# Weight slots, weight halves and work tiles moved to other places modulo 256 bytes in a one-core two-block transformer

## The chip, the cores and the metric

The kernel runs on one core of one Trainium2 chip, in one launch. The metric is the device time of that core in microseconds (us). A profiled execution gives one trace; the plain times are from executions of the same program.

## The reference

Two transformer blocks of depth 2 follow each other on one sequence of 256 tokens and width 1024, all in float32. Cut to the order of the sublayers:

```python
def first_block(x, ...):                     # layer 0 even, layer 1 odd
    mix = even_mixer(...) or odd_mixer(...)  # mLSTM + neighbourhood, or differential attention
    x = layer_norm(ALPHA * x + mix)
    x = layer_norm(ALPHA * x + memory_cross_attention(x, mem, wq, wkv, wo))   # 4 heads of 256
    x = layer_norm(ALPHA * x + swiglu(x, w_gu, w_down))                       # hidden 2816
def second_block(x, ...):                    # twice
    x = layer_norm(ALPHA * x + 0.5 * swiglu_ffn(x, w_in, w_out))              # hidden 2816
    x = layer_norm(ALPHA * x + mixer_sublayer(...))       # top-k, stick-breaking, convolution, gates
    x = layer_norm(ALPHA * x + memory_cross_attention_2(...))                 # 4 heads of 128
    x = layer_norm(ALPHA * x + 0.5 * swiglu_ffn(x, w_in, w_out))
```

Nearly all arithmetic is products of the 256 activations with weight matrices: 725 units of 128x1024 weights, each used once.

## The kernel before

**Split products.** Every weight and every activation of a large product is held as two parts of a reduced float type, high and low; a product is three matmuls (high by high, low by high, high by low). `Stream._load` brings a unit of 128x1024 float32 by a DMA of SP's queue into one of 4 stage tiles; `Stream._split` makes the parts from it: a cast on ScalarE (L218) for the high half, a subtraction on VectorE (L219) for the low one. Both halves lie in one of 10 slots of the pool `wp`, 8192 bytes each in a partition. The order of all engines' work is written out by the program itself, with a table of pauses; nothing is scheduled by a planner.

**Two operands.** In `matmul(out, a, b)` the first operand stands in TensorE's array (it is loaded by a weight load, engine PEld in the profile), the second streams through it (engine PE). A large matmul here streams 256 or 512 columns against a standing 128x128. While one streams, the load for the next one runs. In the profile's rows the streaming operand is named first (`ps<-xT,w` streams `xT`).

**Who is what.** The large products are of these kinds, and the starts in a partition modulo 256 bytes are those of the built program (all other offsets inside a tile are multiples of 512 bytes):

| product (lines) | streams, at | stands, at | standing minus streaming |
|---|---|---|---|
| units, `unit_group` (L348, L350, L352) | `xT`, 128 | weights, 192 | +64 |
| output projections, `bg_mm` (L417) | weights, 192 | `ph`, `pl`, 0 | +64 |
| memory keys, `kv_k` (L307 to L309, `w` by `w`, 256 columns) | memory, 192 | weights, 192 | 0 |
| memory values, `kv_v` (`w` by `w`, 512 columns) | weights, 192 | memory, 192 | 0 |
| `vproj` (512 columns), first step of `ffn` (256 columns) | weights, 192 | `xT`, 128 | -64 |
| branches of `mixer` (`ph` by `w`) | `ph`, `pl`, 0 | weights, 192 | -64 |

`xT` holds the two parts of the activations, 8 blocks of 256 columns each; `ph` and `pl` are the two parts of an intermediate, in tiles of the pool `a1` (35 tiles of 1 KB, tag `k1`), which also holds most other small work tiles.

**The feed-forward sublayer** (`ffn`, six times) matters most below. Four units of the first step come first; one pair of hidden blocks is turned by transposes (L595). Then `for j in range(2, 22)` takes two units of 24 matmuls (gate and up), makes `h` and its parts, and for 16 of the `j` also one block of the output projection with the parts of two steps before (`bg_both`, 24 matmuls of L417 over five accumulators, three of them 512 columns wide). In the first such block each of these three is opened by one 512-wide matmul, so that it has 21 matmuls; all others of these blocks are 256 wide:

```python
for c in [lo] if start or stop else range(lo, hi, 256):
    e = hi if start or stop else c + 256
    mm(acc[:, c - lo:e - lo], p, z[:, c:e], start=start, stop=stop)
```

The last six blocks are held back for `bg_tail`, where the sublayer's normalisation runs between them.

Of the kernel before, what the change touches and what calls it, by code (L numbers as in the profile page):

```python
# [9 lines left out]
F32 = mybir.dt.float32  # L10
F32R = mybir.dt.float32r
# [156 lines left out]

class Blank:


# [16 lines left out]
class Stream:  # L190
# [20 lines left out]
    def _split(self):  # L211
        n = self.net
        cols = self.plan[self.split][2]
        w = self.stage.pop(self.split)
        both = n.wp.tile([128, 2048], F32R, tag="w2", name="w2")
        hi, lo = both[:, :1024], both[:, 1024:]
        self._low()
        n.nc.scalar.copy(hi[:, :cols], w[:, :cols])  # L218
        self.due = lambda: n.nc.vector.tensor_sub(lo[:, :cols], w[:, :cols], hi[:, :cols].bitcast(F32))  # L219
        self.parts[self.split] = (hi, lo)  # L220
        self.split += 1
        self.live += 1
# [44 lines left out]
class Net:  # L267
# [1241 lines left out]
    def build(self):  # L1509
        nc, tc = self.nc, self.tc  # L1510
        with ExitStack() as ctx:
            pool = lambda name, bufs, **k: ctx.enter_context(tc.tile_pool(name=name, bufs=bufs, **k))
            self.one = pool("one", 1)
            self.stage = pool("stage", STAGE)
            pad = pool("pad", 1).tile([128, 16], F32, name="pad")
            self.wp = pool("wp", W_SLOTS)
            wide = pool("a2", 18)
            self.act = Multi(pool("a1", 35), wide) if self.real else Blank()
            self.small = SmallMix(pool("sm_col", 24), pool("sm_o", 2)) if self.real else Blank()
            self.psum = pool("psum", 8, space=bass.MemoryType.PSUM)  # L1520
            self.dram = pool("dram", 1, space=bass.MemoryType.DRAM)
            ctx.enter_context(tc.manual_schedule())
            sq = self.one.tile([128, 3, 128], F32, name="sq")
            self.xT = [self.one.tile([128, 8, S], F32R, tag=f"xT{i}", name="xT") for i in range(2)]
            xq = [self.k2(name="xq") for _ in range(4)]
            for u in range(4):
                nc.scalar.dma_start(xq[u], self.a["xT"][u // 2, :, (u % 2) * 512:(u % 2) * 512 + 512]
                                    .rearrange("p (k c) -> p k c", k=2))
            self.xq = xq
            self.ws.start()  # L1530
            nc.sync.dma_start(sq, self.a["c_sq"])
            self.ident, self.negt, self.strict = (sq[:, i, :] for i in range(3))
            self.mhalf = self.one.tile([128, 8], F32, name="mhalf")
            nc.vector.memset(self.mhalf, -0.5)
            self.negone = self.one.tile([128, 128], F32, name="negone")
            nc.vector.memset(self.negone, -1.0)

            subs = [self.even,
                    lambda: self.xattn("x0", "memT", 2, 1),
                    lambda: self.ffn("f0", 2, 2 * ALPHA, 4 * EPS),  # L1540
                    self.odd,
                    lambda: self.xattn("x1", "memT", 2, 4),
                    lambda: self.ffn("f1", 5, 2 * ALPHA, 4 * EPS)]
            for l in range(2):
                b = 6 + 4 * l
                subs += [lambda l=l, b=b: self.ffn(f"h{l}0", b, 4 * ALPHA, 16 * EPS),
                         lambda l=l, b=b: self.mixer(l, b + 1),
                         lambda l=l, b=b: self.xattn(f"y{l}", "memT2", 1, b + 2),
                         lambda l=l, b=b: self.ffn(f"h{l}1", b + 3, 4 * ALPHA, 16 * EPS)]
            if self.start:  # L1550
                for u in range(4):
                    self.x_split(u)
                self.late_loads()
                self.lam_load()
                self.rel_load()
                for _ in self.tables():
                    pass
            for f in subs[self.start:self.stop]:
                f()
            if self.stop < 14:  # L1560
                self.flush()
                for t in range(2):
                    nc.sync.dma_start(self.out[0, t * 128:t * 128 + 128, :], self.x[:, t, :])
# [40 lines left out]
```

## Time and profile before

| | |
|---|---|
| median of 3 runs | 2245.8 us (2245.5 to 2246.91) |
| the profiled execution: its time, its span | 2246.46 us, 2244.7 us |
| TensorE matmuls, share of the span | 98%, 17920 instructions |
| VectorE, ScalarE, GpSimd | 67%, 51%, 9% |
| granted TensorE clock | 0.998 of full speed (2.4 GHz) |
| DMA, share of 16 engines | about 56%, 182 GB/s |

The span is the time from the first to the last instruction of the trace; the time of the execution is 1.8 us longer. Matmuls are pipelined, so the duration of one (some 280 ns) is much longer than the distance from one start to the next, here called the pitch; the pitch is what the time is made of.

### The profile page before, as it was taken

What the parts mean: (1) busy time and instruction counts of PE and PEld (TensorE: products, weight loads), DVE (VectorE), ACT (ScalarE), POOL (GpSimd) and SP (SyncE); (2) the same over time, 40 slices, a digit from 0 to 9 for tenths busy, and PEclk for the clock granted to TensorE, in tenths of its full rate; (3) what the DMA queues carried; (4) which work ended last, traced back from release to release, by engine and by line L of the source; (5) the groups of instructions that cost most, each with busy time, mean ns of one, the idle gap of its engine ahead of it and who ended that gap; (6) DMA issues with size and microseconds to landing.
All of it is one profiled execution on the core that took longest, in us unless ns stands there. A gap on an engine that the chain in (4) does not pass through costs nothing.

```text
span 2244.7 us, 43647 instructions
## 1 busy us (share of the span) xinstructions
PE 2207.1 (98%) x17920; PEld 2127.7 (95%) x17920; DVE 1498.5 (67%) x2270; ACT 1154.3 (51%) x1844; POOL 203.1 (9%) x239
## 2 busy tenths in 40 slices
PE   8999999999999999999999999999999999999998
PEld 6999999998989999999899999999999999998998
DVE  5885666676657667656587667657656587677665
ACT  4555454378545444444845554444543845545542
POOL 0720000011000000000211100000000101100000
PEclk9999999999999999999999999999999999999999
DMA  7754476463446664764465655764764545554762
GB/s 228 179 170 159 168 256 189 155 209 135 162 152 224 200 188 161 234 189 151 141 182 166 207 179 175 234 191 139 254 190 145 165 153 181 178 193 164 254 191 75
DMA packets 118090, 407.67 MB, mean 182 GB/s; under 512 B 14169, under 2 KB 19418, under 8 KB 117890
## 3 DMA queue, kind: packets, MB, share of 16 engines
q1 hardware_dynamic: 116258, 402.00, 55.0%
q0 software_dynamic: 768, 1.57, 0.9%
q8 instruction: 140, 2.29, 0.4%
q10 hardware_dynamic: 864, 1.31, 0.2%
q14 instruction: 60, 0.49, 0.1%
HBM read 403.76 MB, written 1.06 MB: 180 GB/s over the span
## 4 chain that ended last, share of the span: by engine, by line
PE 84%; DVE 4%; ACT 4%; DMA 4%; issue 2%; POOL 1%; ACTq 0%; SPq 0%; DVEq 0%; POOLq 0%
PE acc L417 21%; PE ps L348 15%; PE ps L350 14%; PE ps L352 14%; PE ps L307 4%; PE ps L309 4%; PE ps L308 4%; DVE w L219 2%; ACT w L218 2%; PE ps L558 1%; PE ps L737 1%; DMA w<-in_o_qk 1%; DMA xq<-in_xT 1%; PE ps L757 1%; ACT qr L1115 0%
## 5 line engine op out<-in xcount | busy, mean ns | idle before, releaser
L219 DVE TENSOR_TENSOR w<-w,w 128x1024 fp32r<-128x1024 f32 x725 | 885.6, 1240 | 364.4 <-ACT w L218 360.5
L348 PE MATMUL ps<-xT,w 128*128 128x256 f32 x3232 | 903.0, 279 | 0.0
L350 PE MATMUL ps<-xT,w 128*128 128x256 f32 x3232 | 896.5, 277 | 0.0
L352 PE MATMUL ps<-xT,w 128*128 128x256 f32 x3232 | 896.1, 277 | 0.0
L218 ACT CAST w<-w 128x1024 fp32r<-128x1024 f32 x725 | 748.6, 1050 | 232.2 <-PE ps L352 121.7
L348 PEld LDWEIGHTS ps<-xT,w 128*128 128x128 f32 x3232 | 607.2, 188 | 8.1 <-issue 5.1
L352 PEld LDWEIGHTS ps<-xT,w 128*128 128x128 f32 x3232 | 608.9, 188 | 0.0
L350 PEld LDWEIGHTS ps<-xT,w 128*128 128x128 f32 x3232 | 607.5, 188 | 0.6
L417 PE MATMUL acc<-w,ph 128*128 128x256 f32 (+1 forms) x2966 | 496.9, 283 | 2.1 <-ACT ph L292 1.5
L417 PEld LDWEIGHTS acc<-w,ph 128*128 128x128 f32 x2966 | 421.1, 189 | 7.6 <-ACT ph L292 2.3
L417 PE MATMUL acc<-w,pl 128*128 128x256 f32 (+1 forms) x1462 | 330.1, 284 | 2.3 <-DVE pl L293 2.3
L417 PEld LDWEIGHTS acc<-w,pl 128*128 128x128 f32 x1462 | 238.5, 189 | 2.7 <-DVE pl L293 2.7
L529 POOL TENSOR_TENSOR col<-col,mhalf 128x1 f32<-128x1 f32 (+1 forms) x38 | 28.6, 751 | 1554.7 <-DVE col L537 1308.3
L570 ACT ACTIVATE k<-ps 128x256 f32<-128x256 f32 x120 | 46.0, 383 | 155.7 <-PE ps L352 155.6
L292 ACT CAST ph<-k 128x256 fp32r<-128x256 f32 x120 | 48.8, 406 | 133.4 <-DVE k L572 133.4
L307 PE MATMUL ps<-w,xT 128*128 128x256 f32 (+1 forms) x304 | 102.0, 336 | 9.2 <-ACT w L218 9.2
L308 PE MATMUL ps<-w,xT 128*128 128x256 f32 (+1 forms) x304 | 99.5, 327 | 1.2 <-DVE w L219 1.2
L571 DVE SCALAR_TENSOR_TENSOR k<-k,ps 128x256 f32<-128x256 f32 x120 | 50.4, 420 | 75.0 <-ACT k L570 74.9
L309 PE MATMUL ps<-w,xT 128*128 128x256 f32 (+1 forms) x304 | 99.3, 327 | 0.0
L307 PE MATMUL ps<-w,w 128*128 128x256 f32 (+1 forms) x288 | 96.0, 333 | 0.0
L544 ACT ACTIVATE x<-x,col 128x512 f32<-128x512 f32 x28 | 20.3, 724 | 141.1 <-POOL col L529 109.5
L309 PE MATMUL ps<-w,w 128*128 128x256 f32 (+1 forms) x288 | 91.9, 319 | 0.0
(259 smaller groups left out, 2268.4 us busy)
## 6 DMA issues: line engine op xcount, KB each, us to landing
w<-in_h_g SPq DMA_DIRECT2D x160, 512.0 KB, 4.5
w<-in_h_d SPq DMA_DIRECT2D x88, 512.0 KB, 4.5
w<-in_f_g SPq DMA_DIRECT2D x80, 512.0 KB, 4.4
w<-in_m_gate SPq DMA_DIRECT2D x48, 512.0 KB, 4.2
w<-in_f_d SPq DMA_DIRECT2D x44, 512.0 KB, 4.5
gb<-in_ln_row SPq DMA_DIRECT2D x28, 512.0 KB, 6.9
w<-in_m_c SPq DMA_DIRECT2D x24, 512.0 KB, 3.5
w<-in_m_br SPq DMA_DIRECT2D x24, 512.0 KB, 3.9
```

What stands on the lines that cost most here:

```text
L218: n.nc.scalar.copy(hi[:, :cols], w[:, :cols])
L219: self.due = lambda: n.nc.vector.tensor_sub(lo[:, :cols], w[:, :cols], hi[:, :cols].bitcast(F32))
L292: nc.scalar.copy(hi, src)
L307: mm(ps, a[0], b[0], start=first, stop=False)
L308: mm(ps, a[0], b[1], start=False, stop=False)
L309: mm(ps, a[1], b[0], start=False, stop=last)
L348: mm(ps, ws[i][0][:, k, :], xh[:, k, :], start=k == 0, stop=False)
L350: mm(ps, ws[i][1][:, k, :], xh[:, k, :], start=False, stop=False)
L352: mm(ps, ws[i][0][:, k, :], xl[:, k, :], start=False, stop=k == 7)
L417: mm(acc[:, c - lo:e - lo], p, z[:, c:e], start=start, stop=stop)
L570: nc.scalar.activation(h, pg, AF.Tanh, scale=0.5)
L571: nc.vector.scalar_tensor_tensor(h, in0=h, scalar=1.0, in1=pg, op0=OP.add, op1=OP.mult)
```

## The change

The spacer of 64 bytes ahead of the weight slots goes. A slot grows from 8192 to 8448 bytes, 33 times 256. In a slot the halves begin at its start, or, for units of the names in `BESIDE`, 64 bytes further. `a1` has 34 tiles for 35. No operation is added or taken away, and on every engine the built program has the same instructions in the same order; only some waits of ScalarE and VectorE in the gate stage of `mixer` (L1418, L1378, L292, L293, L218) name an earlier or later release of a work tile, about 50 in all.

```diff
+HALF = 16
+BESIDE = {"b", "a", "g", "qk", "q", "k", "qa", "ckv", "iq", "ik", "s", "c", "gate", "t"}
+def beside(name):
+    return name.split("_", 1)[-1] in BESIDE
...
-        both = n.wp.tile([128, 2048], F32R, tag="w2", name="w2")
-        hi, lo = both[:, :1024], both[:, 1024:]
+        off = HALF if beside(self.plan[self.split][0]) else 0
+        both = n.wp.tile([128, 2048 + 4 * HALF], F32R, tag="w2", name="w2")
+        hi, lo = both[:, off:off + 1024], both[:, off + 1024:off + 2048]
...
-            pad = pool("pad", 1).tile([128, 16], F32, name="pad")
             self.wp = pool("wp", W_SLOTS)
             wide = pool("a2", 18)
-            self.act = Multi(pool("a1", 35), wide) if self.real else Blank()
+            self.act = Multi(pool("a1", 34), wide) if self.real else Blank()
```

In the built program the slots begin at 128 modulo 256, the `a1` tiles at 192; `xT` stays at 128. The table of above becomes:

| product | streams, at | stands, at | standing minus streaming, before and now |
|---|---|---|---|
| units | `xT`, 128 | weights, 192 | +64, +64 |
| output projections | weights, 128 | `ph`, `pl`, 192 | +64, +64 |
| memory keys | memory, 128 | weights, 192 | 0, +64 |
| memory values | weights, 128 | memory, 128 | 0, 0 |
| `vproj` | weights, 128 | `xT`, 128 | -64, 0 |
| first step of `ffn` | weights, 192 | `xT`, 128 | -64, -64 |
| branches of `mixer` | `ph`, `pl`, 192 | weights, 128 | -64, -64 |

Between two products the load of the next one's standing operand runs while the last matmul of the one before streams. From a unit to an output block that pair was 128 and 0 (+128) and is now 128 and 192 (+64); from an output block to a unit it was 192 and 192 (0) and is now 128 and 192 (+64). Seen modulo 512, all slots lay alike before; now every second slot lies 256 bytes off the others.

## Rows read from the trace of the kernel before

**Rows 1.** Page: the span, and busy time, share and instructions by engine.

```profile
span 2244.7 us, 43647 instructions
PE 2207.1 (98%) x17920; PEld 2127.7 (95%) x17920; DVE 1498.5 (67%) x2270; ACT 1154.3 (51%) x1844; POOL 203.1 (9%) x239
```

**Rows 2.** TensorE's waits: total us, times, longest; first and last of 15.

```profile
PE ps L307 <- ACT w L218: 9.2, 2, 7.2
...
PE ps L1104 <- ACT oz L1100: 0.2, 1, 0.2
```

**Rows 3.** Groups of matmuls by line and shape: count, busy us, mean ns.

```profile
L348 PE MATMUL ps<-xT,w 128*128 128x256 f32 x3232 | 903.0, 279 | 0.0
...
L307 PE MATMUL ps<-w,w 128*128 128x256 f32 x192 | 56.2, 293 | 0.0
...
L307 PE MATMUL ps<-w,xT 128*128 128x512 f32 x112 | 47.0, 420 | 9.2 <-ACT w L218 9.2
```

**Rows 4.** L348 in two stretches: count, min/median/max ns, first and last start.

```profile
L348 PE MATMUL ps<-xT,w x60: 276/276/276, 408.4 to 428.5; 128*128 128x256 f32 x60
...
L348 PE MATMUL ps<-xT,w x45: 281/281/281, 469.8 to 485.4; 128*128 128x256 f32 x45
```

**Rows 5.** Timeline: first and last L348 of both (in the second, 44th).

```profile
408.42 0.28 PE L348 MATMUL ps<-xT,w 128*128 128x256 f32 x1
...
428.48 0.28 PE L348 MATMUL ps<-xT,w 128*128 128x256 f32 x1
...
469.83 0.28 PE L348 MATMUL ps<-xT,w 128*128 128x256 f32 x1
...
485.02 0.28 PE L348 MATMUL ps<-xT,w 128*128 128x256 f32 x1
```

**Rows 6.** Timeline: twelve memory keys, then ten each of vproj and memory values.

```profile
118.71 0.28 PE L307 MATMUL ps<-w,w 128*128 128x256 f32 x1
...
120.03 0.28 PE L309 MATMUL ps<-w,w 128*128 128x256 f32 x1
...
455.06 0.39 PE L307 MATMUL ps<-w,xT 128*128 128x512 f32 x1
...
457.12 0.39 PE L307 MATMUL ps<-w,xT 128*128 128x512 f32 x1
...
202.82 0.39 PE L307 MATMUL ps<-w,w 128*128 128x512 f32 x1
...
204.86 0.39 PE L307 MATMUL ps<-w,w 128*128 128x512 f32 x1
```

**Rows 7.** L417: an output block of ffn, then a stretch of another tail.

```profile
L417 PE MATMUL acc<-w,ph x12: 281/281/281, 330.3 to 332.2; 128*128 128x256 f32 x12
...
L417 PE MATMUL acc<-w,ph x24: 276/276/276, 152.8 to 156.7; 128*128 128x256 f32 x24
```

**Rows 8.** The two units behind that output block (333:337.8), by line.

```profile
L348 PE MATMUL ps<-xT,w 128*128 128x256 f32 x15 | 4.1, 276 | 0.0
```

**Rows 9.** First block: behind its first, second and third wide matmul (280.2:282.7).

```profile
L417 PE MATMUL acc<-w,pl 128*128 128x256 f32 x2 | 0.4, 276 | 0.0
...
L417 PE MATMUL acc<-w,pl 128*128 128x256 f32 x2 | 0.4, 281 | 0.0
...
L417 PE MATMUL acc<-w,ph 128*128 128x256 f32 x6 | 1.1, 281 | 0.0
```

**Rows 10.** Loop of ffn behind its first block, two of six: length, matmuls.

```profile
282.74:428.82 146.08, 146.08 (x1275) 1.00 0.66 215
...
696.03:842.11 146.08, 146.08 (x1274) 1.00 0.68 214
```

**Rows 11.** Gate stage of the first mixer (1167:1280), by line and shape.

```profile
L350 PE MATMUL ps<-xT,w 128*128 128x256 f32 x186 | 51.7, 278 | 0.0
```

**Rows 12.** L1418: ScalarE's idle time before it; who waited (us, times).

```profile
  PE ps L352: 25.5, 25
...
  PEld ps L307: 0.7, 2
```

## The prediction

> **What bounds the kernel now.** The page comes first. TensorE's matmuls fill 98% of the span, VectorE 67%, ScalarE 51% [rows 1]. The list of waits says how much of the rest could be had back: TensorE waits 15 times for someone, from 9.2 us down to 0.2 us, 30 us in all [rows 2]. So neither DMA nor the engines that split the weights set the time; the pitch of 17920 matmuls does, on average 2244.7/17920 = 125 ns. The change does not touch their number or order, so it can act only on the pitch, or through the few waits that it moves.
>
> The next view is one line in two stretches that nothing interrupts. The same instruction, L348, with the same shape and the same starts modulo 256 (streaming at 128, standing at 192), takes 276 ns each time in one stretch and 281 ns each time in the other [rows 4]. The timeline gives the pitches [rows 5]: 20.06 us over 59 x 3 = 177 matmuls is 113.3 ns; 15.19 us over 43 x 3 = 129 is 117.8 ns. I call these the quick and the slow step. The reader is to see the minimum, median and maximum: 60 of 60 alike, 45 of 45 alike. A uniform stretch does not change its step by itself; whichever it comes in with, it keeps. The duration tells which it is.
>
> Third, the places where the step does change. In the loop of `ffn` an output block (L417) runs at 281 ns, yet elsewhere the same line runs 24 times at 276 ns [rows 7], so L417 is not slow by nature. The two units behind the block are at 276 ns again [rows 8]. So in each round the step turns slow on entering the output block and quick on leaving it. These are the places where the distance of the two operands modulo 256 is another for one matmul: +128 on entering, 0 on leaving, +64 everywhere else. The first block shows a third kind of place: behind its first 512-wide matmul the step is quick, behind the second slow, behind the third slow [rows 9]. A wide matmul met in the quick step leaves the slow one, and one met in the slow step leaves the slow one; the first differs, but there the +128 came just before.
>
> **The change, part by part.**
>
> *Output blocks and units.* After the change, entering and leaving have +64 as well, and all of it lies at 128 and 192, where L348 shows both steps holding [rows 4]. What turned the step slow on entering is gone, and so is what turned it quick on leaving. Then the step of the whole loop is decided once, in the first block. There the first wide matmul is met quick (without the +128 ahead of it) and should leave the slow step, as the second one does now; the second and third keep it. If the units before came in slow, the result is the same. Behind this block no 512-wide matmul follows until the tail, so I expect the rest of the loop to stay slow.
>
> The price: behind its first block the loop has 19 x 48 + 15 x 24 = 1272 matmuls (19 pairs of units, 15 output blocks); the window of 146.08 us counts three more that overlap its ends [rows 10]. That is 114.84 ns each, and the second loop has the same length to 0.01 us, as do three more. All slow: 1272 x 117.8 = 149.8 us, 3.75 us more. All quick: 1272 x 113.3 = 144.1 us, 1.95 us less. For six feed-forward sublayers: +22.5 or -11.7 us. I take +22.5. The first block itself has the same mixture and the tail is entered slow either way: nothing for either.
>
> *Memory keys.* Both operands lie alike (0) and the pitch is 1.32 us over 11, 120.0 ns [rows 6]. There are 3 x 192 = 576 such matmuls [rows 3]. At +64 they are at one of the two steps: 576 x 2.2 = 1.3 us gained if slow, 576 x 6.7 = 3.9 us if quick. I take the middle, -2.5 us.
>
> *`vproj`.* Its distance goes from -64 to 0. It has 2.06 us over 9, 228.9 ns, now; memory values, also 512 wide and at 0, have 2.04 over 9, 226.7 ns [rows 6]. 3 x 112 = 336 matmuls [rows 3] by 2.2 ns: -0.7 us. The other bound is no gain. Memory values, the first step of `ffn` and the branches keep their distance: nothing.
>
> *Units outside the loops.* 3 x 3232 [rows 3] less 6 x 912 leaves 4224. Where they follow branches, attention or stalls, either step may hold, and the change alters some of what precedes them. In the gate stage their mean is 278 ns [rows 11], so 2 parts in 5 are slow. All quick would be 4224 x 0.4 x 4.5 = -7.6 us, all slow 4224 x 0.6 x 4.5 = +11.4 us. Nothing says which way; I take zero and keep both ends.
>
> *34 tiles and the moved waits.* About 50 waits of ScalarE and VectorE in the two gate stages change their releaser, among them GpSimd's additions. ScalarE is idle before L1418 for 25.5 us because it waits for TensorE's unit itself, and TensorE has lost 0.7 us to it [rows 12]. That idle time hides a work tile released a round or two earlier. Were the cover gone, the branch matmuls behind that activation would wait; I take zero, and twice the present loss, 1.4 us, as the other end.
>
> *The splits.* Casts and subtractions write to other places; VectorE and ScalarE have a third and a half of the span free [rows 1]. Zero.
>
> Sum: 22.5 - 2.5 - 0.7 = +19.3 us. Against the profiled execution's own time (span 2244.7 and 1.8 around it, 2246.5) that is 2265.8; the median of the runs lies 0.7 below that execution, so 2265. Slower by 0.9%. A measurement of this kernel tells about 0.2%, 4.5 us, from no change.
>
> The Trainium skill, in "SBUF — State Buffer", section "Who interferes with whom", gives TensorE two independent read ports, one for the streaming operand and one for the weight load, and says that "PE and ACT never wait on anyone". By that rule where operands lie cannot matter, and the sum would be zero, 2246 us. The rows differ: 113.3, 117.8 and 120.0 ns for the same shape [rows 5, 6]; the measurement decides here, though that the place causes the difference is my reading of them.
>
> **The rivals.**
>
> *The loop locks quick: 2230 us, faster.* The mechanism is the same, with one step the other way: the wide matmuls of the first block, met at the new places, leave the quick step behind. Then each loop saves 1.95 us, 11.7 us in six; memory keys at the quick step give 3.9 and `vproj` 0.7: 2245.8 - 16.3 = 2229.5. For it: L417 can hold the quick step [rows 7], and one wide matmul did leave it quick [rows 9]. Against it: the second, met quick, did not. It decides at one point, the step of the matmuls right behind the third wide one.
>
> *Places repeat over more than 256 bytes: about 2248.* All slots lie alike modulo 512 now; with a slot of 33 times 256 bytes every second one lies 256 off. If that counts, every new unit is a place where the step can change, and distances come up that no row of this trace shows. With half the matmuls of the loops at either step, the mean is 115.55, 7632 x 0.7 = +5.3 us; less the 3.2 us of the keys and `vproj`, +2. The ends are wide: -11.7 from the loops if all is quick, and 7632 x (120.0 - 114.84) = +39 if all is as the keys are now. It falls to either side.
>
> *The place does not matter, and both steps have another cause: 2246.* For it: the same places show both steps [rows 4]. Against it: the change of step falls on the same places in each round, and five loops have the same length within 0.01 us.
>
> **How the numbers follow.** The forecast gets 0.57, the quick lock 0.22, the longer repeat 0.15, no effect 0.06. The longer repeat is split evenly over the three signs. Slower: 0.57 + 0.05 = 0.62; within 0.2%: 0.06 + 0.05 = 0.11; faster: 0.22 + 0.05 = 0.27. The forecast's own range is 2257 to 2274: the units outside the loops down 7.6 or up by most of 11.4. The full range goes down to 2234: it holds the forecast, no effect, most of the longer repeat and the upper edge of the quick lock; what is left out is most of the quick lock, about 0.2.
>
> **What would show it.** In the changed trace the units inside the `ffn` loops at 281 ns where they are 276 now, the output blocks at 281 as before, and loops of 149.8 us; memory keys no longer at 120 ns; the same short list of waits. The prediction is wrong if these units are at 276 ns: then either the first block leaves the quick step, or something other than the distance modulo 256 turns it. It is wrong in its premise if the step changes from unit to unit with every second slot.

## The result, and the profile after

The changed kernel takes 2269.78 us (median of 4 runs, 2266.15 to 2271.47) against 2246.36 us before; the ratio is 1.0102 [1.0084, 1.0119], so it is slower by 1.0%. Its profiled execution took 2270.8 us. One execution below, the profiled one of `z2_two_uniform_zero`, ran at a granted clock of 0.817 and took 2514.82 us; it is left out of that kernel's time, and its trace is not used. Ten lines were added above the products, so L348, L350, L352 are now L358, L360, L362, L417 is L427, and L307 to L309 are L317 to L319.

The page and the list of TensorE's waits (first and last of 15) come first. They answer to [rows 1, 2].

```profile
span 2269.1 us, 43641 instructions
...
PE 2229.1 (98%) x17920; PEld 2149.9 (95%) x17920; DVE 1498.5 (66%) x2270; ACT 1153.9 (51%) x1844; POOL 204.3 (9%) x239
```

```profile
PE ps L317 <- ACT w L228: 8.2, 2, 7.4
...
PE ps L1250 <- ACT sp L1188: 0.3, 1, 0.3
```

The span is 24.4 us longer and TensorE is as full as before, with the same number of matmuls. The 15 waits sum to 32.2 us against 30.0, which is 2.2 us of the difference. The rest is pitch, and the question is where it grew and by what. The six loops of `ffn`, from behind the first output block to the tail, answer to [rows 10]; the columns are length, TensorE's busy time and matmuls, granted clock, DMA share, GB/s:

```profile
281.36:431.18 149.82, 149.82 (x1275) 1.00 0.65 209
...
2094.98:2244.79 149.81, 149.81 (x1274) 1.00 0.60 193
sum 898.89, PE 898.89; mean PE 149.81
```

They sum to 898.9 us against 6 x 146.08 = 876.5 before, 22.4 us more. All the rest is 2269.1 - 898.9 = 1370.2 us against 2244.7 - 876.5 = 1368.2. In the loops the granted clock is full in both.

Outside the loops it is not. In the changed kernel's trace the granted clock falls to half (1.2 GHz) for 3.4 us at four places, in that of the kernel before at one, apart from the last microseconds of each. Two of the four, then the one of the kernel before, with the same columns as above:

```profile
1360.01:1363.42 3.41, 3.41 (x17) 0.50 0.89 316
...
2059.74:2063.15 3.41, 3.41 (x18) 0.50 0.78 299
...
20.85:24.26 3.41, 3.41 (x9) 0.50 0.82 279
```

In these stretches a 256-wide matmul takes 213 ns from start to start and not 113 to 118, and a 512-wide one 427 and not 227 to 236. Summed over the matmuls in them, the four cost some 6.4 us (3.1 in output blocks, 2.0 in units, 1.2 in branches), and the one of the kernel before cost 1.7, all in its first `vproj`. So about 4.7 of the 24.4 us are clock and not pitch at full clock. That the change brings these drops is not shown: the other traces have them in differing numbers, and `w3_three_uniform_wide`, as slow in its loops, has only one, at 19.5 us. Of the four executions of the changed kernel the one with the highest granted clock, 0.999, took 2266.15 us; the others, at 0.996 to 0.998, took 2268.77 to 2271.47.

Inside the first loop every unit of L358 has the duration of the slow step (count, minimum/median/maximum ns); the output blocks have it too, 281/281/281 of 242 and of 121:

```profile
L358 PEld LDWEIGHTS ps<-xT,w x304: 192/192/192, 281.2 to 430.7; 128*128 128x128 f32 x152
L358 PE MATMUL ps<-xT,w x304: 281/281/281, 281.4 to 430.8; 128*128 128x256 f32 x152
```

This also shows something I had not read before: the weight load of L358 takes 192 ns each time, while the groups of weight loads in the same window give the other two of the three matmuls 188 ns.

```profile
L358 PEld LDWEIGHTS ps<-xT,w 128*128 128x128 f32 x304 | 58.4, 192 | 0.0
L360 PEld LDWEIGHTS ps<-xT,w 128*128 128x128 f32 x304 | 57.1, 188 | 0.0
L362 PEld LDWEIGHTS ps<-xT,w 128*128 128x128 f32 x304 | 57.1, 188 | 0.0
```

So the slow step is not a uniform slowness: one weight load in three is 4 ns longer, always the same of the three. In the quick step all are 187 or 188 ns (the loop with one matmul ahead of the wide one, below). This mark is what the experiments came down to.

The first output block, ahead of this loop, answers to [rows 9]: the units before it (277.4 to 278.5 us), then its first wide matmul and those behind it (278.83 to 279.2). The wide one is met in the quick step and leaves the slow one.

```profile
L358 PE MATMUL ps<-xT,w 128*128 128x256 f32 x4 | 1.1, 276 | 0.0
...
L427 PE MATMUL acc<-w,pl 128*128 128x256 f32 x2 | 0.4, 281 | 0.0
L427 PE MATMUL acc<-w,ph 128*128 128x512 f32 x1 | 0.4, 388 | 0.0
```

The groups of the whole span answer to [rows 3], and the timeline of memory keys and of `vproj` (first and last of ten matmuls each) to [rows 6]:

```profile
L358 PE MATMUL ps<-xT,w 128*128 128x256 f32 x3232 | 911.8, 282 | 0.0
...
L317 PE MATMUL ps<-w,w 128*128 128x256 f32 x192 | 55.5, 289 | 0.0
...
L317 PE MATMUL ps<-w,xT 128*128 128x512 f32 x112 | 45.7, 408 | 8.3 <-ACT w L228 8.2
```

```profile
117.97 0.28 PE L317 MATMUL ps<-w,w 128*128 128x256 f32 x1
...
119.03 0.28 PE L317 MATMUL ps<-w,w 128*128 128x256 f32 x1
...
457.35 0.39 PE L317 MATMUL ps<-w,xT 128*128 128x512 f32 x1
...
459.39 0.39 PE L317 MATMUL ps<-w,xT 128*128 128x512 f32 x1
```

Memory keys left the 120.0 ns pitch: 1.06 us over 9 is 117.8 ns, the slow step. In this stretch `vproj` went from 228.9 to 2.04 us over 9 = 226.7 ns, as forecast.

### The profile page after: what moved, and what is told of

Read it like the earlier page. It is cut to its first block, busy times and chain, and to the rows that moved or that the text cites. A ratio compares the mean times of both kernels' runs of the same rounds, so it can differ in the third digit from the quotient of the medians.

```text
span 2269.1 us, 43641 instructions
## 1 busy us (share of the span) xinstructions
PE 2229.1 (98%) x17920; PEld 2149.9 (95%) x17920; DVE 1498.5 (66%) x2270; ACT 1153.9 (51%) x1844; POOL 204.3 (9%) x239
## 3 DMA queue, kind: packets, MB, share of 16 engines
HBM read 403.76 MB, written 1.06 MB: 178 GB/s over the span
## 4 chain that ended last, share of the span: by engine, by line
PE 86%; DVE 4%; ACT 4%; DMA 2%; issue 2%; POOL 1%; SPq 0%; ACTq 0%; DVEq 0%; POOLq 0%
PE acc L427 22%; PE ps L358 15%; PE ps L360 15%; PE ps L362 15%; PE ps L317 5%; PE ps L319 4%; PE ps L318 4%; DVE w L229 2%; ACT w L228 1%; PE ps L568 1%; PE ps L747 1%; DMA xq<-in_xT 1%; PE ps L767 1%; DMA rb<-rbt 0%; PE ps L663 0%
## 5 line engine op out<-in xcount | busy, mean ns | idle before, releaser
L358 PE MATMUL ps<-xT,w 128*128 128x256 f32 x3232 | 911.8, 282 | 0.0
L360 PE MATMUL ps<-xT,w 128*128 128x256 f32 x3232 | 905.5, 280 | 0.0
L362 PE MATMUL ps<-xT,w 128*128 128x256 f32 x3232 | 905.2, 280 | 0.0
L358 PEld LDWEIGHTS ps<-xT,w 128*128 128x128 f32 x3232 | 616.5, 191 | 8.1 <-issue 4.8
L360 PEld LDWEIGHTS ps<-xT,w 128*128 128x128 f32 x3232 | 608.5, 188 | 0.7 <-DVE w L229 0.2
L362 PEld LDWEIGHTS ps<-xT,w 128*128 128x128 f32 x3232 | 608.4, 188 | 0.0
L427 PE MATMUL acc<-w,ph 128*128 128x256 f32 (+1 forms) x2966 | 499.4, 284 | 2.1 <-ACT ph L302 1.5
L427 PEld LDWEIGHTS acc<-w,ph 128*128 128x128 f32 x2966 | 424.7, 190 | 7.6 <-ACT ph L302 2.3
L427 PE MATMUL acc<-w,pl 128*128 128x256 f32 (+1 forms) x1462 | 330.9, 285 | 2.3 <-DVE pl L303 2.3
L427 PEld LDWEIGHTS acc<-w,pl 128*128 128x128 f32 x1462 | 239.0, 189 | 2.7 <-DVE pl L303 2.7
L317 PE MATMUL ps<-w,xT 128*128 128x256 f32 (+1 forms) x304 | 100.7, 331 | 8.3 <-ACT w L228 8.2
L318 PE MATMUL ps<-w,xT 128*128 128x256 f32 (+1 forms) x304 | 98.2, 323 | 3.0 <-DVE w L229 3.0
L319 PE MATMUL ps<-w,xT 128*128 128x256 f32 (+1 forms) x304 | 98.2, 323 | 0.0
L317 PE MATMUL ps<-w,w 128*128 128x256 f32 (+1 forms) x288 | 95.3, 331 | 0.0
L319 PE MATMUL ps<-w,w 128*128 128x256 f32 (+1 forms) x288 | 91.3, 317 | 0.0
```

The source lines that it names most:

```text
L317: mm(ps, a[0], b[0], start=first, stop=False)
L318: mm(ps, a[0], b[1], start=False, stop=False)
L319: mm(ps, a[1], b[0], start=False, stop=last)
L358: mm(ps, ws[i][0][:, k, :], xh[:, k, :], start=k == 0, stop=False)
L360: mm(ps, ws[i][1][:, k, :], xh[:, k, :], start=False, stop=False)
L362: mm(ps, ws[i][0][:, k, :], xl[:, k, :], start=False, stop=k == 7)
```

## The experiments

**The theory** after this result: the step of a loop is set by the places where the distance or the width of a matmul differs, and the change took away, at each output block, the place that turned the step quick. **The rivals**: the loss has another source than the loops; or the distance is of no account and a step is only carried along. All kernels below are the changed kernel with an edit. The product of an extra matmul is overwritten by the unit behind it. A time without a ratio is that of a single execution.

*The old places in the loops* (`e4_old_loops`). It gives the blocks' weights and `ph`, `pl` their old places modulo 256 (192 and 0), and with them the branches' weights and the other work tiles of `a1`; it leaves the slots, the keys, `vproj` and the 34 tiles changed.

```diff
-BESIDE = {..., "gate", "t"}
+BESIDE = {..., "gate", "t", "d", "o", "br"}
...
+            pad = pool("pad", 1).tile([128, 16], F32, name="pad")
```

> The changed kernel with the places in the feed-forward loops, the output projections and the branches as before (weights of output projections and branches 64 bytes further, a spacer of 64 bytes ahead of the work tiles: 192 and 0); memory keys, vproj, the slots of 8448 bytes and the 34 work tiles stay as changed. My theory: the loops are 146.08 us again; with memory keys (1.3 to 3.9 us less) and vproj (0.7 us less) the kernel is at 2243 us, from 2238 to 2250 by the units outside the loops. Rival (the time was lost elsewhere: by the wider slots, by 34 tiles and their waits, by vproj): 2265 us or more, and only the feed-forward loops' few microseconds come back.

Measured: 2247.45 us, ratio to the kernel before 1.0001 [0.9991, 1.0011]. The groups of its first loop (283.37 to 429.46 us, 146.09 long):

```profile
L358 PE MATMUL ps<-xT,w 128*128 128x256 f32 x304 | 84.1, 277 | 0.0
...
L427 PE MATMUL acc<-w,ph 128*128 128x256 f32 x242 | 40.3, 281 | 0.0
```

Units quick and blocks slow again, and all six loops are back at 146.08 us. The whole loss goes with the places that this edit puts back, and in the loops these are those of the output blocks; slots of 8448 bytes, 34 tiles and the moved waits cost nothing that this interval can tell. That the loops come back says that these places matter, not yet in which way: a step that the old places turn, or a price of the new places themselves. `w1_uniform_wide` below tells the two apart. The gain of the keys that I expected on top did not show either; TensorE's waits sum to 32.4 us in this kernel too, 2.4 more than before, and matmuls at half clock cost some 4.1 us, 2.4 more than before; each is of the size of that gain, but one profiled execution of each doesn't settle it.

*Units at distance 0* (`e3_units_zero`): every half begins at its slot's start.

```diff
 def beside(name):
-    return name.split("_", 1)[-1] in BESIDE
+    return False
```

> The changed kernel with every weight at the start of its slot: units stream at 128 and stand at 128, distance 0 in place of +64; output blocks, values, vproj and branches keep their places, memory keys go back to distance 0, the first step of the feed-forward goes to 0. Theory, a distance of 0 has a step of its own as memory keys had before (120.0 ns): units 120.0 ns each, loops 912 x 120.0 + 360 x 117.8 = 151.9 us, and outside the loops the units that were quick lose 6.7 ns and the slow ones 2.2 ns, some 19 us: about 2300 us. Rival, the distance does not matter and the step is only carried along: loops 149.8 us or 144.1 us, 2270 or 2235 us.

Measured: 2294.27 us. The six loops are 151.83 or 151.84 us each. Groups of the first (283.82 to 435.65):

```profile
L358 PE MATMUL ps<-xT,w 128*128 128x256 f32 x304 | 86.0, 283 | 0.0
...
L358 PEld LDWEIGHTS ps<-xT,w 128*128 128x128 f32 x304 | 58.4, 192 | 0.0
L360 PEld LDWEIGHTS ps<-xT,w 128*128 128x128 f32 x304 | 58.4, 192 | 0.0
L362 PEld LDWEIGHTS ps<-xT,w 128*128 128x128 f32 x304 | 58.4, 192 | 0.0
```

The loop comes out to 0.1 us: at distance 0 every load of the units takes 192 ns, not one in three, and their pitch is 120.0 ns, neither of the two steps. The distance counts by itself, and the rival falls. The estimate for the rest was too high: outside its loops the kernel lost 11.4 us to the changed one (2292.6 - 911.0 = 1381.6 against 1370.2), or some 14 when the half-clock stretches of both traces are taken out, and not 19 and the keys' 1.3.

*Units at distance +128* (`e7_units_far`): `HALF` is 32, so that their weights, and those of the other names in `BESIDE`, lie at 0 modulo 256 (the slot keeps its 8448 bytes).

> The changed kernel with the units' weights 128 bytes behind the start of their slot in place of 64: units stream at 128 and stand at 0, a distance of +128 that no uniform stretch has shown. Output blocks keep +64. Theory, +128 is a place that turns the step slow, as on entering an output block in the kernel before: units and loops slow everywhere, 149.8 us a loop, and the units outside that are quick now lose 4.5 ns each, about 10 us: 2280 us. Rival, a step of its own between the two or quick: 113.3 ns for the units gives loops of 912 x 113.3 + 360 x 117.8 = 145.7 us and 2245 us or less.

Measured: 2271.95 us, loops of 149.18 or 149.19 us. Groups of the first:

```profile
L358 PE MATMUL ps<-xT,w 128*128 128x256 f32 x304 | 85.5, 281 | 0.0
...
L358 PEld LDWEIGHTS ps<-xT,w 128*128 128x128 f32 x304 | 57.2, 188 | 0.0
...
L427 PE MATMUL acc<-w,ph 128*128 128x256 f32 x241 | 39.2, 277 | 0.0
```

Neither theory was right. The output blocks are quick, and the units have an uneven step of their own: with 360 block matmuls at 113.3 ns, 149.18 us leaves 118.9 ns for each of the 912. Yet their loads take 188 ns. Distance +128 costs in another way than distance 0, and does not simply turn the step slow, as I had put it.

*One extra matmul behind the first block* (`e1_one_extra`, `e5_extra_uniform`, `e6_extra_and_wide`). If a place at distance 0 turns the step quick, one for each `ffn` should give the whole loop back. The first streams the part that its standing operand is cut from (distance 0); the second streams `xT` (+64, as all others), as a control; the third is the first with a 512-wide matmul before `j` = 12 added. `extra` is the high part `ph` of the last output block.

```diff
+            if j == 3:
+                nc.tensor.matmul(pg, extra[:, 0:128], extra, start=True, stop=True)  # e1, e6
+                nc.tensor.matmul(pg, extra[:, 0:128], self.xT[0][:, 0, :], start=True, stop=True)  # e5 instead
+            if j == 12:  # e6 alone
+                nc.tensor.matmul(ps.rearrange("p a b -> p (a b)"), extra[:, 0:128],
+                                 self.xT[0][:, 0:2, :].rearrange("p a b -> p (a b)"), start=True, stop=True)
```

> The changed kernel with one more matmul in each of the six feed-forward sublayers, behind the first output block and ahead of the next unit: it streams a part at 192 while the next load stands at 192, so that there is one place of distance 0, as on leaving each output block in the kernel before. Its product is overwritten by the unit that follows. My theory (a step is kept while the distance is +64 throughout, and one place of distance 0 turns the slow step quick): units and output blocks of the loops at 276 ns, loops of 1272 x 113.3 = 144.2 us for 149.8, so 34 us less than the changed kernel: 2236 us. Rival (the loops are slow because weights and parts now lie at 128 and 192 in output blocks too, not because of the step that they came in with): loops stay at 149.8 us, and the time is that of the changed kernel plus six extra matmuls, 2270.5 us.

> Control for the run with one more matmul: the same extra matmul at the same point, but it streams the first block of the activations at 128, so that the distance stays +64 everywhere. Its product is overwritten by the unit that follows. My theory: nothing turns, the loops stay at 281 ns in all matmuls and last 149.9 us; six extra matmuls cost 0.7 us, 2270.5 us. Rival (any extra matmul there, by its delay or its accumulator, turns the step): loops of 144.3 us, 2237 us.

> The run with one more matmul of distance 0, and in each feed-forward sublayer at j = 12 a second extra matmul, 512 columns wide, at distance +64. Both products are overwritten by the units that follow. My theory (a wide matmul met in the quick step leaves the slow one): the loops are quick, 276 ns, from j = 3 to j = 11 and slow, 281 ns, from j = 12 on: 648 x 113.3 + 624 x 117.8 + 0.3 = 147.2 us each, 2.6 us less than in the changed kernel, 2254 us. Rival (the width does not matter, the slow step came from something else in the first block): quick to the end, 144.5 us each, 2238 us.

Measured: 2270.92 us for the first, ratio 1.0099 [1.0082, 1.0115], and 2270.86 for the control; both have loops of 149.93 us, all slow, the control as expected. A place at distance 0 does not turn the step merely by being there; the theory fell in that form. The first came out at its rival's number, so at this point the rival, a price of the new places themselves, still stood. The third took 2252.69 us with loops of 147.40, and in the opposite order to what I expected: slow up to the wide matmul, quick behind it. L358 before and behind it, and the wide matmul (L614) with its load, in two stretches of the first loop (282.27 to 358, 358 to 429.67):

```profile
L358 PE MATMUL ps<-xT,w 128*128 128x256 f32 x144 | 40.5, 281 | 0.0
...
L358 PE MATMUL ps<-xT,w 128*128 128x256 f32 x160 | 44.2, 276 | 0.0
...
L614 PE MATMUL ps<-xT,ph 128*128 128x512 f32 x1 | 0.4, 394 | 0.0
L614 PEld LDWEIGHTS ps<-xT,ph 128*128 128x128 f32 x1 | 0.2, 188 | 0.0
```

So a wide matmul met in the slow step can leave the quick one, which no row read before had shown [rows 9]. The trace of the kernel before has such places all the same, outside the loops. One is at 248.6 us: the matmuls ahead of it (247.9 to 248.5), the wide one with its load, the matmuls behind it (249.2 to 250.3).

```profile
L417 PE MATMUL acc<-w,ph 128*128 128x256 f32 x6 | 1.0, 281 | 0.0
...
L417 PE MATMUL acc<-w,pl 128*128 128x512 f32 x1 | 0.4, 393 | 0.0
...
L417 PEld LDWEIGHTS acc<-w,pl 128*128 128x128 f32 x1 | 0.2, 188 | 0.0
...
L417 PE MATMUL acc<-w,ph 128*128 128x256 f32 x9 | 1.5, 276 | 0.0
```

*Where in the period of three the wide matmul falls* (`w0_wide`, `w1_uniform_wide`, `w2_two_uniform_wide`, `w3_three_uniform_wide`). The wide matmul stands before `j` = 3, with 0, 1, 2 or 3 extra matmuls of the usual distance ahead of it. The expectations, here and for distance 0 below, count four matmuls too many between the first block's third wide matmul and the extra one: they say 14 to 17, the trace has 10 to 13, which leaves their differences as they are.

```diff
+            if j == 3:
+                nc.tensor.matmul(pg, extra[:, 0:128], self.xT[0][:, 0, :], start=True, stop=True)  # 0 to 3 times
+                nc.tensor.matmul(ps.rearrange("p a b -> p (a b)"), extra[:, 0:128],
+                                 self.xT[0][:, 0:2, :].rearrange("p a b -> p (a b)"), start=True, stop=True)
```

> The same with the wide extra matmul alone: 14 matmuls lie between the last wide one and it, 2 modulo 3. Theory of three: nothing turns, loops of 150.05 us at 281 ns, 2271 us. Rival (any wide matmul behind the first block turns the step): loops of 144.4 us, 2238 us.

> The changed kernel with two extra matmuls in each feed-forward sublayer, behind the first output block: one of 256 columns and then one of 512, both streaming the activations at 128 against a part at 192, distance +64. Their products are overwritten by the unit that follows. My new theory: the slow step has a period of three matmuls, and whether a wide matmul (or a place of distance 0) turns it quick hangs on which of the three it meets. In the run where a wide matmul at j = 12 turned the loops quick, 14 + 1 + 648 = 663 matmuls lay between the last wide one of the first block and it, 0 modulo 3; here 15 do, 0 as well. So it turns: loops of 1272 x 113.3 + 0.35 = 144.5 us and 2238 us, 32 below the changed kernel and 8 below the one before. Rival (only the long stretch ahead, or its place in the sublayer, let the wide one turn the step): loops of 150.2 us, 2272 us.

> The same with two extra matmuls of 256 columns ahead of the wide one: 16 lie between, 1 modulo 3, as with the second and third wide matmul of the first block (4 between), which do not turn the step. Theory of three: nothing turns, loops of 150.3 us, 2272 us. Rival (any wide matmul turns it, or a longer gap does): loops of 144.6 us, 2239 us.

> The changed kernel with three extra matmuls of the same places as all others, and then one extra 512-wide matmul, behind the first output block of each feed-forward sublayer: 17 matmuls lie between the block's third wide matmul and the extra wide one (products overwritten, output unchanged). Seen so far with the wide one: 14 between leaves the loop slow, 15 and 16 turn it quick. Theory A, the count modulo three decides: 17 stands as 14, the loops stay slow, 150.2 us each, 2271 us. Rival, it needs more than 14 between: turned, loops 144.8 us, about 2237 us.

Measured, with the duration of the wide matmul and of its own weight load (the same in all six loops, to 1 ns):

| extra ahead | time, us | first loop, us | behind it | wide, ns | its load, ns |
|---|---|---|---|---|---|
| 0 | 2269.36 | 150.05 | slow | 398 | 192 |
| 1 | 2235.13 | 144.52 | quick | 394 | 187 |
| 2 | 2236.31 | 144.63 | quick | 392 | 188 |
| 3 | 2272.36 | 150.40 | slow | 398 | 192 |

The rows with none ahead (L612 the wide matmul; 280.77 to 430.82), then those with one ahead (L613; 281.43 to 425.95):

```profile
L358 PE MATMUL ps<-xT,w 128*128 128x256 f32 x304 | 85.4, 281 | 0.0
...
L612 PE MATMUL ps<-xT,ph 128*128 128x512 f32 x1 | 0.4, 398 | 0.0
L612 PEld LDWEIGHTS ps<-xT,ph 128*128 128x128 f32 x1 | 0.2, 192 | 0.0
```

```profile
L358 PE MATMUL ps<-xT,w 128*128 128x256 f32 x304 | 83.9, 276 | 0.0
...
L358 PEld LDWEIGHTS ps<-xT,w 128*128 128x128 f32 x304 | 57.1, 188 | 0.0
...
L427 PE MATMUL acc<-w,ph 128*128 128x256 f32 x242 | 39.2, 276 | 0.0
...
L613 PE MATMUL ps<-xT,ph 128*128 128x512 f32 x1 | 0.4, 394 | 0.0
...
L613 PEld LDWEIGHTS ps<-xT,ph 128*128 128x128 f32 x1 | 0.2, 187 | 0.0
```

The kernel with one ahead shows a whole loop in the quick step, units and output blocks, at the places of the changed kernel, so these places have no price of their own: 144.52 us less the two extra ones (0.35 us from start to start) is 144.17, 113.3 ns for each of the 1272. With one and with three ahead the theory of the count modulo three held, three ahead against its rival; with two it fell, since I had read the first block's own wide matmuls as the case that stays slow.

The load tells which do: they stay slow wherever the wide matmul's own load is the long one of the three. In the first block the second and third wide matmul stand behind one wide and four narrow ones. If a wide one counts as two, that is six, a multiple of three, and so are 2 + 10 and 2 + 13 here; 2 + 11 and 2 + 12 are not. In the trace of the changed kernel the loads of the first block agree: those of the second and the third wide matmul take 192 ns, and those of the four narrow ones behind each take 187 or 188.

I formed this rule after these runs, and no run was made to test it. The traces can test it, since each has many wide matmuls in its output blocks. In the 13 traces taken near full clock I count those of L417 or L427 and the extra ones that have four 256-wide matmuls on either side, one step in the three ahead, and no half-clock stretch near:

| the wide matmul is met | its own load | in 13 traces | of these, the kernel before | behind it |
|---|---|---|---|---|
| slow | 192 ns | 487 | 39 | slow, all |
| slow | 187 or 188 ns | 119 | 6 | quick, all |
| quick | 187 or 188 ns | 238 | 11 | slow, all |

There is no exception, and the kernel before had all three cases on record.

With one extra ahead the changed kernel is faster than the kernel before: 0.995 [0.9935, 0.9965] of its time.

*The same for distance 0* (`z2_two_uniform_zero`, `z1_uniform_zero`): the extra matmul at distance 0 with two or one of the usual ones ahead; none ahead is `e1_one_extra`.

```diff
+            if j == 3:
+                nc.tensor.matmul(pg, extra[:, 0:128], self.xT[0][:, 0, :], start=True, stop=True)  # once or twice
+                nc.tensor.matmul(pg, extra[:, 0:128], extra, start=True, stop=True)
```

> The changed kernel with three extra matmuls of 256 columns at the same point: two of distance +64 and then the one of distance 0 that did not turn the step when it stood alone. Products are overwritten. In the kernel before, the matmul of distance 0 that turns the step behind the first block follows the last wide one after 13 others, 1 modulo 3; alone it followed after 14; here after 16, 1 again. Theory of three: it turns, loops of 144.2 + 0.35 = 144.5 us, 2238 us. Rival (leaving the output block turned the step before for another reason than the place of distance 0): loops of 150.2 us, 2272 us.

> The changed kernel with one extra matmul of the usual places and then one at distance 0 (it streams the part that its standing operand is cut from), 15 matmuls behind the first block's third wide matmul (products overwritten, output unchanged). At 14 between such a matmul left the loop slow, at 16 it turned it quick. Theory A, the count modulo three decides, and a distance-0 matmul turns at the same counts as a wide one: quick, loops about 144.5 us, 2236 us. Rival, it turns at one count of three alone: slow, loops 150.0 us, 2271 us.

Measured: two ahead 2238.23 us, ratio 0.9961 [0.9947, 0.9975], turned, as its time tells; one ahead 2275.26 us, loops of 150.05, still slow. A place at distance 0 turns the step too, but here at one position in three: none ahead (its load 192 ns) and one ahead (188 ns) fail. That it takes the same two positions as a wide one, as theory A had it, is wrong.

Position is not all of it either. In the kernel before, leaving an output block turned the step in each of the 96 rounds. Behind the first block (6 rounds) the first load of the unit is the long one; in the other 90 it is the second. The loads around the first and the second leaving of the first loop (282.65 to 282.72, 290.95 to 291.1):

```profile
L348 PEld LDWEIGHTS ps<-xT,w 128*128 128x128 f32 x1 | 0.2, 192 | 0.0
...
L350 PEld LDWEIGHTS ps<-xT,w 128*128 128x128 f32 x1 | 0.2, 192 | 0.0
...
L348 PEld LDWEIGHTS ps<-xT,w 128*128 128x128 f32 x1 | 0.2, 187 | 0.0
```

In the run with one ahead the last long loads lie two and five loads before the unit's first one, just as in these 90 rounds, and its loops did not turn. So for distance 0 something else counts as well, and it stays open.

## Why the prediction was right

The time, 2269.8 us, lies within the forecast's own range, 4.8 us above the forecast of 2265. The loops lost what the forecast said, for the reason it gave; what lies above is, in the profiled executions, mostly clock, which the sum did not have.

*The loops.* Forecast 149.8 us each and +22.5; measured 149.81 and +22.4. With the old places in the loops the whole loss is gone, and with the new places and an irregular matmul at the right position the loops are quick, 144.5 us. The two together show the cause: the change took away the places that turned the step quick, and the new places as such cost nothing in the loops. The sentence that carried the forecast, "the first wide matmul is met quick ... and should leave the slow step", was right. The other one, "one met in the slow step leaves the slow one", was too general, and six wide matmuls in the trace of the kernel before were against it. The first block's second and third wide matmul keep the slow step because their own load is the long one, and the prediction did not ask for that; in this step it had luck.

*The quick lock* was therefore a real case and not a mere chance of the draw: one extra narrow and one wide matmul give it, at 2235.1 us, where the rival was worked out at 2230. The difference is mostly the extra matmuls (6 x 0.35 = 2.1 us) and the keys, which gained 1.3 us there where the rival had them quick, at 3.9.

*The clock.* The two spans differ by 24.4 us. The half-clock stretches cost 4.7 us more in that of the changed kernel; without them 19.7 are left, where the sum had 19.3. Part of this nearness is luck too, since the terms below miss in both directions.

*Keys and `vproj`.* Summed from each start to the next, the 576 memory keys went from 72.9 to 71.6 us, -1.3 where -2.5 was taken: that is the bound of the slow step, 2.2 ns each. `vproj` went from 86.7 to 85.0, but 1.7 us of the 86.7 are the half-clock stretch of the kernel before, which also lifts the mean duration of L307's 112 by some 6 of its 420 ns [rows 3]. In the 192 matmuls of `vproj` behind the first one, which have neither such a stretch nor a wait, the gain is 0.2 us, 1 ns each, where 2.2 was taken: the stretch of [rows 6] does not stand for them all.

*Units outside the loops.* In the same sums the units inside the loops went from 622.4 to 644.5 us, and the 4224 outside from 505.0 to 507.6, +2.5, where zero was taken between -7.6 and +11.4. Of that, 2.0 are half clock. The output blocks outside the loops went up by 2.2 us, and 3.1 are half clock, so at full clock they gained 1.0, which the sum did not have.

*Waits and tiles.* Zero was taken, and up to 1.4 us from L1418. The list is as short as before, and the weight loads, which had lost 0.7 us to L1418 [rows 12], lose 0.3. Others grew: L318's for VectorE's half from 1.2 to 3.0 us, all in the first `vproj` (one of them at 23 us, where the trace of the kernel before ran at half clock), and L1379's for `rb` from 1.0 to 2.8. Whether the slots, the tiles, the shifted times or the clock did that was not tried.

*The longer repeat over 512 bytes* is refuted as a cause of changes in the loops: with every second slot 256 bytes off, all 304 matmuls of L358 in a loop read 281 ns.

*No effect of the place* is refuted by the units at distance 0: 283 ns and 2294 us. By the rule of the Trainium skill ("SBUF — State Buffer", "Who interferes with whom") that was put beside the sum, the changed kernel and the two with units at distance 0 and +128, which all have the arithmetic of the kernel before, would have taken 2246 us. The measurements, 2270, 2294 and 2272 us, decide.

## What to carry to other kernels

When a kernel is one long row of equal matmuls, read the pitch and the durations of matmuls and weight loads by stretch, with minimum, median and maximum: two steps 4% apart can hide in one mean, and the one that a loop comes in with it may keep to its end. A change that makes all places alike takes away what turns the step back as well as what turns it; look for the last irregular matmul ahead of the loop and for where it falls among the long loads, since here that decided. Where the same instruction runs at two steps, try an extra matmul or two ahead of the loop: here a narrow and a wide one for each loop, 0.35 us long, made it 5.3 us shorter. And before a remainder of a few microseconds is put down to pitch, take out the stretches at a lower granted clock.

## What the runs showed of the hardware

- For the same 128x256 matmul at full granted clock, three steady pitches: 113.3 ns with all weight loads at 187 or 188 ns, 117.8 ns with one load of three at 192, 120.0 ns with all at 192. The first two hold for over a thousand matmuls at the same places; the third came with streaming and standing operand at the same start modulo 256.
- The position of the long load within the three moves with each extra matmul (L358 in the changed kernel, L362 with one more), and three more bring it back: L360 with none and with three ahead of the wide one.
- A wide matmul met in the slow step whose own load is a long one leaves the slow step as it is (398 ns for it, 487 of 487); at the other two positions it turns it quick (394 and 392 ns, 119 of 119). One met in the quick step turns it slow (238 of 238).
- A distance-0 matmul turned the changed kernel's loops at one position of three; in the kernel before, the change of distance on leaving a block turned them at two.
- In a stretch at 1.2 GHz granted clock a 256-wide matmul took 213 ns from start to start; one such stretch of 3.4 us costs this kernel some 1.6 us.
- Not settled: why a period of three, what distance +128 does (uneven pitches near 118.9 ns, loads of 188 or 189 ns), and what beside its position makes a place of distance 0 turn the step.
